# A softmax with relative position bias: chunks of three rows in eight buffers for chunks of four in six, and one store near the end issued later

## The chip, the cores and the metric

The kernel runs on one core of one Trainium2 chip. The metric is the device time of one execution in microseconds (us), lower is better. The core has five engines with instruction queues of their own; here VectorE (DVE in the profile) adds, inverts and scales, ScalarE (ACT) does the exponentials and issues the stores, SyncE (SP) issues the loads, GpSimd (POOL) makes two small index tables. Sixteen DMA engines carry out the transfers of both queues: loads on queue q1, stores on queue q10.

## The reference

```python
B, H, S = (2, 8, 2112); max_rel = 16
rel = clip(pos[:, None] - pos[None, :], -16, 16) + 16
logits = logits + rel_bias[:, rel][None]        # (2, 8, 2112, 2112) fp32
logits = logits - logits.max(axis=-1, keepdims=True)
exp = np.exp(logits)
out = exp / exp.sum(axis=-1, keepdims=True)
```

Each of the 2 x 8 x 2112 rows of 2112 numbers gets a bias that depends only on column minus row, clipped to 16 either way, and then a softmax over the row. 285.5 MB are read and as many written.

## The kernel before

**Tiling.** The rows are spread over 128 partitions: each of the 16 (batch, head) pairs has 8 partitions, and each partition has T = 264 rows that follow one another in memory. A chunk is R = 4 rows of every partition, one contiguous run of 4 x 8448 = 33,792 bytes in each. There are N = 66 chunks. BUFS = 6 buffers `L[u]` hold them; chunk n is in buffer n % 6, is changed in place and is stored from there. The bias comes from one strip `F` of 2375 numbers per partition, made once at the start: row after row reads it at an offset one smaller.

**What happens to a chunk.** SP issues the load (`load`, line 91), which counts up `loaded[u]` by 16 when it has landed. DVE waits for that (`vec`, line 126), adds the strip to rows 0 and 1 in one instruction and to rows 2 and 3 in a second (`add`, line 116; HALF = 2). After each, ACT does two exponentials whose sums go to `tot[u]` (`exps`, line 123). DVE waits for a pair's sums, takes the reciprocals (line 137) and scales the two rows (line 141), then the other pair. It counts up `scaled` once per chunk. ACT, which has gone on to `store` (line 95) after its fourth exponential, waits for `scaled` and issues the store, which counts up `stored[u]`. SP waits for `stored[u]` before it loads chunk n + 6 into the same buffer (`reload`, line 99). No row maximum is subtracted.

**What sets the order.** Every engine goes through the chunks in order, in a hardware loop of BUFS chunks per pass (`passes`, line 145) and the remainder unrolled. All waits are semaphores written out by hand: `take` (line 87) waits and subtracts. ACT's queue therefore reads: exponentials of n, wait for the scaling of n, store n, exponentials of n + 1. DVE's reads: wait for load n, both adds of n, wait for sums, first pair, wait for sums, second pair, wait for load n + 1.

**Start and end.** Chunk 0 is loaded in pieces (four quarters of row 0, then single rows; `FIRST`, line 66), so that the first bytes come early. The last buffer serves as scratch for making the strip, so its first load waits for `made`. The last chunk, 65, is loaded in two halves with a semaphore each (line 231), and DVE and ACT store it in two halves too; in `vec`, both adds of that chunk still come ahead of both scalings. SP ends by waiting for the last stores.

Of the kernel before, what the change touches and what calls it, by code (L numbers as in the profile page):

```python
# [14 lines left out]
def kernel(  # L15
# [18 lines left out]
    P = 128  # L34
    B, H, S, S2 = logits.shape
# [4 lines left out]
    T = S // Q  # L40
    assert Q * B * H == P and T * Q == S and T % W == 0
    M = T // W
    R = 4
    HALF = 2
    BUFS = 6
    N = T // R
    assert N * R == T
    FW = S + T - 1
    NB = (FW - 2 * MR) // W
    assert NB * W + 2 * MR == FW  # L50
    RS = R * S

    const = ctx.enter_context(tc.tile_pool(name="const", bufs=1))
    F = const.tile([P, FW], FP32, tag="F", name="F")
    rbP = const.tile([P, W], FP32, tag="rbP", name="rbP")
    L = [const.tile([P, RS], FP32, tag=f"L{u}", name=f"L{u}") for u in range(BUFS)]
    tot = [const.tile([P, R], FP32, tag=f"tot{u}", name=f"tot{u}") for u in range(BUFS)]


    qi, mm, qm, eq, lt, gt, rest = (  # L60
        L[BUFS - 1][:, NB * m : NB * (m + 1)] for m in range(7)
    )
# [3 lines left out]
    FIRST = [(S * m // 4, S * (m + 1) // 4) for m in range(4)]  # L66
    FIRST += [(S * m, S * (m + 1)) for m in range(1, R)]

    def rows(t, start, run=RS):
        return bass.AP(  # L70
            tensor=t.tensor, offset=t.offset + start * S, ap=[[T * S, P], [1, run]]
        )

    section = ctx.enter_context(tc.tile_critical(name="rows"))  # L74
    loaded = [nc.alloc_semaphore(f"loaded{u}") for u in range(BUFS)]
    stored = [nc.alloc_semaphore(f"stored{u}") for u in range(BUFS)]
    table = nc.alloc_semaphore("table")
    blocks_ready = nc.alloc_semaphore("blocks_ready")
    strip = nc.alloc_semaphore("strip")
    late = nc.alloc_semaphore("late")  # L80
# [6 lines left out]
    def take(eng, sem, v):  # L87
        eng.wait_ge(sem, v).then_inc(sem, -v)  # L88

    def load(eng, u, start):  # L90
        eng.dma_start(out=L[u][:], in_=rows(logits, start)).then_inc(loaded[u], 16)

    def store(eng, u, start, r0=0, r1=R):
        take(eng, scaled, 1)
        eng.dma_start(
            out=rows(out, start + r0, (r1 - r0) * S), in_=L[u][:, r0 * S : r1 * S]
        ).then_inc(stored[u], 16)

    def reload(eng, u, start):
        take(eng, stored[u], 16)  # L100
        load(eng, u, start)

    def add(eng, u, s0, start):
        x = L[u]
        x3 = bass.AP(
            tensor=x.tensor,
            offset=x.offset + (s0 + HALF - 1) * S,
            ap=[[list(x.ap[0])[0], P], [-S, HALF], [1, S]],
        )

        F3 = bass.AP(
            tensor=F.tensor,
            offset=(F.offset + T - HALF - s0) - start,
            ap=[[list(F.ap[0])[0], P], [1, HALF], [1, S]],
        )
        eng.tensor_tensor(out=x3, in0=x3, in1=F3, op=ALU.add).then_inc(added, 1)  # L116

    def exps(eng, u):
        for s0 in range(0, R, HALF):
            take(eng, added, 1)  # L120
            for i in range(s0, s0 + HALF):
                x = L[u][:, i * S : (i + 1) * S]
                e = eng.activation(out=x, in_=x, func=EXP, accum_out=tot[u][:, i : i + 1])  # L123
            e.then_inc(summed, 1)

    def vec(eng, u, start, halves=()):

        if not halves:
            take(eng, loaded[u], 16)
        for h, s0 in enumerate(range(0, R, HALF)):  # L130
            if halves:
                take(eng, halves[h], 16)
            add(eng, u, s0, start)
        for s0 in range(0, R, HALF):
            take(eng, summed, 1)
            t = tot[u][:, s0 : s0 + HALF]
            eng.reciprocal(out=t, in_=t).then_inc(inverted, 1)  # L137
            take(eng, inverted, 1)
            for i in range(s0, s0 + HALF):
                x = L[u][:, i * S : (i + 1) * S]  # L140
                e = eng.tensor_scalar_mul(out=x, in0=x, scalar1=tot[u][:, i : i + 1])  # L141
            if halves or s0 + HALF == R:
                e.then_inc(scaled, 1)

    def passes(eng, n0, n1, body):

        k = (n1 - n0) // BUFS * BUFS
        with eng.Fori(n0 * R, (n0 + k - BUFS) * R + 1, BUFS * R) as i:
            for u in range(BUFS):
                body((n0 + u) % BUFS, i + u * R)  # L150
        for n in range(n0 + k, n1):
            body(n % BUFS, n * R)
# [44 lines left out]
    def table_load(eng, bs):  # L197
        for b in bs:
            eng.dma_start(
                out=rbP[b * H * Q : (b + 1) * H * Q],  # L200
                in_=bass.AP(
                    tensor=rel_bias.tensor,
                    offset=rel_bias.offset,
                    ap=[[W, H], [0, Q], [1, W]],
                ),
            ).then_inc(table, 16)

    with nc.Block() as block:  # L208

        @block.sync  # L210
        def _(eng):


            for c0, c1 in FIRST:
                eng.dma_start(
                    out=L[0][:, c0:c1],
                    in_=bass.AP(
                        tensor=logits.tensor,
                        offset=logits.offset + c0,
                        ap=[[T * S, P], [1, c1 - c0]],  # L220
                    ),
                ).then_inc(loaded[0], 16)
            for u in range(1, BUFS):
                if u == BUFS - 1:
                    take(eng, made, 1)
                load(eng, u, u * R)
            passes(eng, BUFS, N - 1, lambda u, start: reload(eng, u, start))
            u = (N - 1) % BUFS
            take(eng, stored[u], 16)
            for s0, sem in ((0, loaded[u]), (HALF, late)):  # L230
                eng.dma_start(
                    out=L[u][:, s0 * S : (s0 + HALF) * S],
                    in_=rows(logits, (N - 1) * R + s0, HALF * S),
                ).then_inc(sem, 16)
            for n in range(N - BUFS, N - 1):
                take(eng, stored[n % BUFS], 16)
            take(eng, stored[u], 16 * R // HALF)

        @block.gpsimd
        def _(eng):  # L240
            eng.iota(qi, pattern=[[0, NB]], base=0, channel_multiplier=M).then_inc(  # L241
                blocks_ready, 1
            )
            eng.iota(mm, pattern=[[1, NB]], base=1 - M, channel_multiplier=0).then_inc(  # L244
                blocks_ready, 1
            )

        @block.scalar
        def _(eng):
            table_load(eng, range(B))  # L250

            def whole(u, start):
                exps(eng, u)
                store(eng, u, start)

            whole(0, 0)
            passes(eng, 1, N - 1, whole)
            u = (N - 1) % BUFS
            exps(eng, u)
            for s0 in range(0, R, HALF):  # L260
                store(eng, u, (N - 1) * R, s0, s0 + HALF)

        @block.vector
        def _(eng):
            strip_of(eng)
            eng.wait_ge(loaded[0], 16 * len(FIRST)).then_inc(loaded[0], 16 - 16 * len(FIRST))
            passes(eng, 0, N - 1, lambda u, start: vec(eng, u, start))
            u = (N - 1) % BUFS
            vec(eng, u, (N - 1) * R, halves=(loaded[u], late))


# [28 lines left out]
```

## Time and profile before

| | |
|---|---|
| Median of 6 runs | 1337.84 us |
| Lowest and highest | 1330.35 and 1351.61 us |
| Profiled execution, device time | 1355.03 us |
| Its span in the profile | 1353.3 us |
| DVE busy | 954.9 us, 539 instructions |
| ACT busy | 529.5 us, 529 instructions |
| Bytes moved | 571.00 MB, 422 GB/s over the span |
| ACT waiting for DVE ahead of exponentials | 788.4 us in 130 waits |
| DVE waiting ahead of adds | 262.5 us in 61 waits |

The times in the profile come from one execution. Its page gives busy time per engine, the span in 40 equal slices of 33.8 us (the busy share of an engine as a digit, and the GB/s that the DMA engines moved), the DMA queues with packets, megabytes and share of time, groups of equal instructions (line, engine, operation, output and input, count; busy us, mean ns of one; idle time just before them and who ended it), and the DMA issues (count, KB each, median us from issue to landing). A timeline lists instructions with start and duration. A table of stretches gives for each window its width, the busy time of DVE, ACT and POOL, the clock, the mean busy share of the 16 DMA engines and the GB/s. The trace behind it also holds a record of each DMA packet: queue, start, duration and bytes. A packet here is one partition's run of a chunk, or the 4-byte write that counts up a semaphore at the end of a transfer on each of the 16 DMA engines.

### The profile page before, as it was taken

Reading aid. Unit: us, or ns where it says so; the run is one execution under the profiler, and the core shown is the slowest. Engines: PE = TensorE matmul, PEld = TensorE weight load, DVE = VectorE, ACT = ScalarE, POOL = GpSimd, SP = SyncE. Lnnn points to the kernel's source line nnn. Section 1 sums busy time; section 2 is a strip of 40 time slices with the busy share of each in tenths; the row PEclk is TensorE's granted clock in tenths of the full one; section 3 lists DMA queues with packets and bytes.
Section 4 is the critical chain, followed back from the end, with each engine's and each line's share of the span. In section 5 each row is a group of like instructions: output and inputs, shape, how many; then the busy total and the mean of one; then the engine's idle time right before and its main releaser. Section 6 shows DMA issues by size and latency. Waiting matters only on the chain. (4 is left out here: it accounts for less than half of the span.)

```text
span 1353.3 us, 2505 instructions
## 1 busy us (share of the span) xinstructions
DVE 954.9 (71%) x539; ACT 529.5 (39%) x529; POOL 0.5 (0%) x6
## 2 busy tenths in 40 slices
DVE  6887766767767767667667767667667667667673
ACT  2444424424434334334334344244244344244242
POOL 0000000000000000000000000000000000000000
DMA  9999999999999999999999999999999999999975
GB/s 387 428 432 433 432 432 433 430 432 432 429 427 433 428 430 432 427 430 428 430 428 430 430 433 431 431 432 431 434 433 432 434 435 431 427 431 432 428 328 238
DMA packets 20307, 571.00 MB, mean 422 GB/s; under 512 B 2384, under 2 KB 2384, under 8 KB 2896
## 3 DMA queue, kind: packets, MB, share of 16 engines
q1 hardware_dynamic: 10512, 285.48, 49.6%
q10 hardware_dynamic: 9792, 285.50, 48.9%
q14 instruction: 3, 0.02, 0.0%
HBM read 285.49 MB, written 285.47 MB: 422 GB/s over the span
## 5 line engine op out<-in xcount | busy, mean ns | idle before, releaser
L123 ACT ACTIVATE L<-L 128x2112 f32<-128x2112 f32 x264 | 516.0, 1955 | 788.4 <-ACTq L88 788.4
L116 DVE TENSOR_TENSOR L<-L,F 128x4224 f32<-128x4224 f32 x132 | 595.8, 4555 | 262.5 <-DVEq L88 262.5
L141 DVE TENSOR_SCALAR L<-L,tot 128x2112 f32<-128x2112 f32 x264 | 336.4, 1316 | 20.0 <-DVEq L88 3.0
L137 DVE RECIPROCAL tot<-tot 128x2 f32<-128x2 f32 x132 | 21.3, 162 | 99.1 <-DVEq L88 99.1
L123 ACT ACTIVATION_READ_ACCUMULATOR L<-L 128x1 f32 x264 | 49.2, 186 | 0.0
L123 ACT ACT_TABLE_LOAD x1 | 1.3, 1283 | 21.6 <-ACTq L88 21.6
L193 DVE TENSOR_TENSOR F<-L,rbP 128x2343 f32<-128x2343 f32 x1 | 2.6, 2601 | 0.1
L194 DVE TENSOR_TENSOR F<-F,L 128x2343 f32<-128x2343 f32 x1 | 2.6, 2600 | 0.1
L185 DVE TENSOR_SCALAR L<-L,rbP 128x71 f32<-128x71 f32 x1 | 0.3, 259 | 3.1 <-DVEq L88 3.1
L180 DVE TENSOR_SCALAR L<-L 128x71 int32<-128x71 int32 x1 | 0.2, 199 | 1.5 <-DVEq L88 1.5
L183 DVE TENSOR_SCALAR L<-L 128x71 f32<-128x71 f32 x3 | 0.6, 198 | 0.5 <-DVEq L88 0.2
L188 DVE SCALAR_TENSOR_TENSOR L<-L,rbP 128x71 f32<-128x71 f32 x1 | 0.3, 294 | 0.2 <-DVEq L88 0.2
L181 DVE TENSOR_TENSOR L<-L 128x71 f32<-128x71 int32 x1 | 0.2, 234 | 0.1
L186 DVE COPY F<-rbP 128x16 f32<-128x16 f32 x1 | 0.2, 175 | 0.1
L192 DVE COPY F<-rbP 128x16 f32<-128x16 f32 x1 | 0.2, 176 | 0.1
L244 POOL IOTA L<- 128x71 int32 x1 | 0.2, 189 | 0.0
L241 POOL IOTA L<- 128x71 int32 x1 | 0.2, 188 | 0.6 <-SPq L74 0.6
L284 POOL MEMSET const-bfloat16-1.0<- 128x1 bf16 x1 | 0.1, 102 | 0.0
L284 POOL MEMSET const-uint8-127<- 128x1 uint8 x1 | 0.1, 102 | 0.0
L284 POOL MEMSET const-float32-0.0<- 128x1 f32 x1 | 0.1, 99 | 0.2 <-issue 0.2
L284 POOL MEMSET const-float32-1.0<- 128x1 f32 x1 | 0.1, 99 | 0.0
## 6 DMA issues: line engine op xcount, KB each, us to landing
out_dram<-L ACTq DMA_DIRECT2D x65, 4224.0 KB, 47.1
L<-in_logits_dram SPq DMA_DIRECT2D x64, 4224.0 KB, 58.4
L<-in_logits_dram SPq DMA_DIRECT2D x2, 2112.0 KB, 60.5
out_dram<-L ACTq DMA_DIRECT2D x2, 2112.0 KB, 9.0
L<-in_logits_dram SPq DMA_DIRECT2D x3, 1056.0 KB, 10.0
L<-in_logits_dram SPq DMA_DIRECT2D x4, 264.0 KB, 3.4
rbP<-in_rel_bias_dram ACTq DMA_DIRECT2D x2, 8.2 KB
```

The costliest lines, as they stand in the source:

```text
L116: eng.tensor_tensor(out=x3, in0=x3, in1=F3, op=ALU.add).then_inc(added, 1)
L123: e = eng.activation(out=x, in_=x, func=EXP, accum_out=tot[u][:, i : i + 1])
L137: eng.reciprocal(out=t, in_=t).then_inc(inverted, 1)
L141: e = eng.tensor_scalar_mul(out=x, in0=x, scalar1=tot[u][:, i : i + 1])
L180: step(eng.tensor_single_scalar(out=qi, in_=qi, scalar=M * Q - 1, op=ALU.bitwise_and))
L181: step(eng.tensor_tensor(out=qm, in0=qi, in1=mm, op=ALU.subtract))
L183: step(eng.tensor_scalar(out=m, in0=qm, scalar1=0.0, scalar2=None, op0=op))
L185: step(eng.tensor_scalar(out=rest, in0=lt, scalar1=low, scalar2=None, op0=ALU.mult))
L188: eng.scalar_tensor_tensor(out=rest, in0=gt, scalar=high, in1=rest, op0=ALU.mult, op1=ALU.add)
L193: step(eng.tensor_tensor(out=blocks, in0=wide(eq), in1=rev, op=ALU.mult))
L194: step(eng.tensor_tensor(out=blocks, in0=blocks, in1=wide(rest), op=ALU.add))
L284: nc = _bacc.Bacc("TRN2", target_bir_lowering=False, num_devices=1)
```

## The change

Chunks have three rows in place of four, so there are 88 of them, in eight buffers in place of six. The two halves of a chunk become `PARTS`: rows 0 and 1, and row 2 alone. Adds, exponentials, reciprocals and scalings follow these parts, and so do the two loads and two stores of the last chunk.

At the end ACT's order is written out. Up to chunk 84 it is as before. The store of chunk 85 (the last but two) isn't issued after its own exponentials: it is handed to `exps` of chunk 86 as `first` and issued there after the wait for chunk 86's first add and ahead of its first exponential. Then follow the store of 86, the exponentials of 87 and its two stores.

```diff
-    R = 4
-    HALF = 2
-    BUFS = 6
+    R = 3
+    PARTS = [(0, 2), (2, R)]
+    BUFS = 8
...
-    def exps(eng, u):
-        for s0 in range(0, R, HALF):
+    def exps(eng, u, first=None):
+        for r0, r1 in PARTS:
             take(eng, added, 1)
-            for i in range(s0, s0 + HALF):
+            if first and r0 == 0:
+                first()
+            for i in range(r0, r1):
...
-        for h, s0 in enumerate(range(0, R, HALF)):
-            if halves:
-                take(eng, halves[h], 16)
-            add(eng, u, s0, start)
-        for s0 in range(0, R, HALF):
+        for m, (r0, r1) in enumerate(PARTS):
+            if parts:
+                take(eng, parts[m], 16)
+            add(eng, u, r0, r1, start)
+        for r0, r1 in PARTS:
             take(eng, summed, 1)
-            t = tot[u][:, s0 : s0 + HALF]
+            t = tot[u][:, r0:r1]
...
-            for s0, sem in ((0, loaded[u]), (HALF, late)):
+            for (r0, r1), sem in zip(PARTS, (loaded[u], late)):
...
-            passes(eng, 1, N - 1, whole)
-            u = (N - 1) % BUFS
+            passes(eng, 1, N - 3, whole)
+
+            u = (N - 3) % BUFS
             exps(eng, u)
-            for s0 in range(0, R, HALF):
-                store(eng, u, (N - 1) * R, s0, s0 + HALF)
+            exps(eng, (N - 2) % BUFS, lambda: store(eng, u, (N - 3) * R))
+            store(eng, (N - 2) % BUFS, (N - 2) * R)
+            exps(eng, (N - 1) % BUFS)
+            for r0, r1 in PARTS:
+                store(eng, (N - 1) % BUFS, (N - 1) * R, r0, r1)
```

More of the change, by code (lines that the diff above doesn't have):

```diff
@@ L101, in reload, with add @@
         load(eng, u, start)
-    def add(eng, u, s0, start):
+    def add(eng, u, r0, r1, start):
         x = L[u]
@@ L106, in add @@
             tensor=x.tensor,
-            offset=x.offset + (s0 + HALF - 1) * S,
-            ap=[[list(x.ap[0])[0], P], [-S, HALF], [1, S]],
+            offset=x.offset + (r1 - 1) * S,
+            ap=[[list(x.ap[0])[0], P], [-S, r1 - r0], [1, S]],
         )
@@ L112, in add @@
             tensor=F.tensor,
-            offset=(F.offset + T - HALF - s0) - start,
-            ap=[[list(F.ap[0])[0], P], [1, HALF], [1, S]],
+            offset=(F.offset + T - r1) - start,
+            ap=[[list(F.ap[0])[0], P], [1, r1 - r0], [1, S]],
         )
         eng.tensor_tensor(out=x3, in0=x3, in1=F3, op=ALU.add).then_inc(added, 1)
-    def exps(eng, u):
-        for s0 in range(0, R, HALF):
+    def exps(eng, u, first=None):
+        for r0, r1 in PARTS:
             take(eng, added, 1)
-            for i in range(s0, s0 + HALF):
+            if first and r0 == 0:
+                first()
+            for i in range(r0, r1):
                 x = L[u][:, i * S : (i + 1) * S]
@@ L124, in exps, with vec @@
             e.then_inc(summed, 1)
-    def vec(eng, u, start, halves=()):
-        if not halves:
+    def vec(eng, u, start, parts=()):
+        if not parts:
             take(eng, loaded[u], 16)
-        for h, s0 in enumerate(range(0, R, HALF)):
-            if halves:
-                take(eng, halves[h], 16)
-            add(eng, u, s0, start)
-        for s0 in range(0, R, HALF):
+        for m, (r0, r1) in enumerate(PARTS):
[3 more added lines that the diff above has]
+        for r0, r1 in PARTS:
             take(eng, summed, 1)
-            t = tot[u][:, s0 : s0 + HALF]
+            t = tot[u][:, r0:r1]
             eng.reciprocal(out=t, in_=t).then_inc(inverted, 1)
             take(eng, inverted, 1)
-            for i in range(s0, s0 + HALF):
+            for i in range(r0, r1):
                 x = L[u][:, i * S : (i + 1) * S]
                 e = eng.tensor_scalar_mul(out=x, in0=x, scalar1=tot[u][:, i : i + 1])
-            if halves or s0 + HALF == R:
+            if parts or r1 == R:
                 e.then_inc(scaled, 1)
@@ L229, in _ @@
             take(eng, stored[u], 16)
-            for s0, sem in ((0, loaded[u]), (HALF, late)):
+            for (r0, r1), sem in zip(PARTS, (loaded[u], late)):
                 eng.dma_start(
-                    out=L[u][:, s0 * S : (s0 + HALF) * S],
-                    in_=rows(logits, (N - 1) * R + s0, HALF * S),
+                    out=L[u][:, r0 * S : r1 * S],
+                    in_=rows(logits, (N - 1) * R + r0, (r1 - r0) * S),
                 ).then_inc(sem, 16)
@@ L236, in _ @@
                 take(eng, stored[n % BUFS], 16)
-            take(eng, stored[u], 16 * R // HALF)
+            take(eng, stored[u], 16 * len(PARTS))
         @block.gpsimd
@@ L268, in _ @@
             u = (N - 1) % BUFS
-            vec(eng, u, (N - 1) * R, halves=(loaded[u], late))
+            vec(eng, u, (N - 1) * R, parts=(loaded[u], late))
 _INS = ['logits', 'rel_bias']
```

## The prediction

> **What bounds the kernel now.** I read the page's busy shares first, then its 40 slices, its queues and issue groups, then stretches of the end, and the timeline at both ends.
>
> ```profile
> DVE 954.9 (71%) x539; ACT 529.5 (39%) x529; POOL 0.5 (0%) x6
> DMA  9999999999999999999999999999999999999975
> GB/s 387 428 432 433 432 432 433 430 432 432 429 427 433 428 430 432 427 430 428 430 428 430 430 433 431 431 432 431 434 433 432 434 435 431 427 431 432 428 328 238
> q1 hardware_dynamic: 10512, 285.48, 49.6%
> q10 hardware_dynamic: 9792, 285.50, 48.9%
> out_dram<-L ACTq DMA_DIRECT2D x65, 4224.0 KB, 47.1
> L<-in_logits_dram SPq DMA_DIRECT2D x64, 4224.0 KB, 58.4
> ```
>
> No engine is full, but the transfers are: 36 slices lie between 427 and 435 GB/s. Loads (q1) and stores (q10) move 571 MB. Loads take 58.4 us from issue to landing and stores 47.1, though one chunk each way passes in 20.4 us (load 6 is issued at 58.6 us, load 65 at 1262.5: 1203.9/59), so 5.2 chunks of transfers are always outstanding. The chain of waits stops after 2.6 us and says nothing.
>
> The two weak slices look like loss: (432-328)/432 and (432-238)/432 of 33.8 us are 8.1 + 15.2 = 23 us. Stretches of the end (width; DVE, ACT, POOL busy; clock; DMA share; GB/s) show whose loss it is:
>
> ```profile
> 1297.00:1317.00 20.00, 14.42 (x9) 8.01 (x8) 0.00 (x0) 1.00 0.66 279
> 1317.00:1325.00 8.00, 4.41 (x1) 3.47 (x3) 0.00 (x0) 1.00 0.95 410
> 1325.00:1331.00 6.00, 0.23 (x1) 0.53 (x2) 0.00 (x0) 1.00 0.50 214
> 1331.00:1335.00 4.00, 4.00 (x1) 0.00 (x0) 0.00 (x0) 1.00 0.06 25
> 1335.00:1338.00 3.00, 2.85 (x4) 2.55 (x3) 0.00 (x0) 1.00 0.08 34
> ```
>
> A share of 0.06 is one DMA engine of 16. In the packet records that engine finishes load 64 at 1300.3 us and the two halves of load 65 at 1315.3 and 1330.3; another is through with them at 1297.6. From 1299 on the late one has no gap: it has eight packets of store 64 left at 1331.6, which last to 1341.5, when store 65's first half (issued 1338.21) is waiting; that takes it to 1346.5, the second half (issued 1342.56) to 1351.5. **The bound is one late DMA engine, busy to the end; the 23 us belong to the other fifteen**, which cannot take over its partitions.
>
> Its own work: a 33,792 B packet takes 1251 ns and the next starts 4 ns before its end, 1247 ns; 16,896 B take 625, 8448 B 315, 2112 B 82 ns in the same way. Per engine: 1032 x 1.247 + 32 x 0.625 + 24 x 0.315 + 32 x 0.082 + 140 completion writes x 0.006 = 1318 us. The first packet starts at 2.0 us, the span ends 1.8 us after the last, 1.7 us lie around the span: **1323.5 us with no packet late**. The profiled execution took 1355.0 (span 1353.3), so its late engine lost 31 us to slow packets, spread over the run (20.4 us per chunk against 16 x 1.247 = 19.95). The median, 1337.84, is 17 below the profiled execution: about 14 us lost.
>
> **The Trainium skill.** "DMA: Bandwidth & Descriptors", section "Where 436 GB/s comes from", puts the ports' ceiling at 435 GB/s; the slices agree (427 to 435). Its section "Queues, rings and completion order" says that each DMA engine takes its queues in turn, packet by packet; the records alternate so wherever both have work. Its section "Latency and other measured facts" says that two engines are usually slower, and suspects GpSimd-issued DMAs; here one is late although none is issued by GpSimd. "VectorE: DVE Perf Modes", section on the TRN2 errata, prices an fp32 tensor_tensor at (N+151)/0.96 ns: 4557 for N = 4224, where the row below has 4555.
>
> **The change part by part.**
>
> *Bytes and packets.* Bytes are the same. A 25,344 B packet lies on the line through the sizes above: 1247 - (1247-315)/3 = 936 ns. Per engine then 1384 x 0.936 (86 loads, 87 stores, 8 packets each) + 16 x 0.625 + 32 x 0.315 + 32 x 0.082 + 183 x 0.006 = 1319 to 1320: **+1 to +2 us**, on the path. Bounds: nothing, if the line is flat, and +7 if slow packets come per packet and not per byte (a third more of some 14 us is +5, added to the +2).
>
> *Compute per chunk.* It must stay below the DMA period, about 0.75 x 20.4 = 15.3 us (14.98 with no packet late).
>
> ```profile
> L123 ACT ACTIVATE L<-L 128x2112 f32<-128x2112 f32 x264 | 516.0, 1955 | 788.4 <-ACTq L88 788.4
> L116 DVE TENSOR_TENSOR L<-L,F 128x4224 f32<-128x4224 f32 x132 | 595.8, 4555 | 262.5 <-DVEq L88 262.5
> L141 DVE TENSOR_SCALAR L<-L,tot 128x2112 f32<-128x2112 f32 x264 | 336.4, 1316 | 20.0 <-DVEq L88 3.0
> L137 DVE RECIPROCAL tot<-tot 128x2 f32<-128x2 f32 x132 | 21.3, 162 | 99.1 <-DVEq L88 99.1
> 50.03 9.02 DVE L116 TENSOR_TENSOR L<-L,F 128x4224 f32<-128x4224 f32 x2
> 66.11 9.02 DVE L116 TENSOR_TENSOR L<-L,F 128x4224 f32<-128x4224 f32 x2
> ```
>
> The last two lines, where DVE never waits for data, give 16.08 us per chunk of four, against 20.4: 4.3 spare. For three rows: two-row add 4.55, hand-over 0.13, two exponentials to 8.7, hand-over 0.14, reciprocal and its wait 0.31, two scalings to 11.6; the one-row add (2357 ns by the formula) fits under the exponentials; the third exponential ends at 10.8, under the scalings; reciprocal and one scaling to **13.2**. Spare: 1.8 to 2.1 us. DVE's sum goes from 955 to 88 x (4.555 + 2.357 + 3 x 1.316 + 2 x 0.162) = 984 us. Cost nothing: covered by the transfers. With the cover gone it would be the rival below.
>
> *Eight buffers of three.* The same 24 rows. In-flight time is 8 x 15.3 - 13.5 = 109 us, before 6 x 20.4 - 16.4 = 106. It splits otherwise. Chunk 0 is in about 2.5 us sooner (14.4) and its store goes out near 28.5 instead of 33.9, so fewer loads have landed by then; when store 0 lands (about 48), 4.2 of 8 loads are in, and the next load waits for 3.8 + 1 chunks: near 70 us for loads, 39 for stores (58 and 47 before). Both queues stay filled; cost nothing. DMA issues (0.35 us each on ACT, 88 in place of 66) lie in ACT's idle time. In the first stretch six small loads go out instead of seven: nothing, the engines are busy behind them.
>
> *The held store.* Chunks 85 to 87 end the run. Store 85's wait for the scaling and its one DMA issue move on ACT behind the wait for chunk 86's first add. Take load 86's landing as 0. Chunk 85's scaling ends near -1.9; the store now goes out at 4.9, **7 us later**. Queued behind it on ACT are the exponentials of 86 (+0.35 us, in DVE's spare time), and nobody waits for stored[5] but SP's last waits, since the last load needs store 79. On its own queue it overtakes nothing, and q1 is not touched. A gap opens only if the late engine runs out of stores before 4.9. Store 84 went out at -17.3 and would land at +21.7, so about 10 packets are left at 0; the two-row load takes 8 of them past by 12.5 us (936 + 625 ns a pair) and they last to about 15. Then 85 and 86 (out at 13.7) are there. The last load is in at 22.5, with 10 store packets left, to 31.9; the two-row part's store is out at 29.2, the last at 30.8. **No gap before, none after: gain 0.** Bounds: -3 us if in the shown runs the margin of 3.3 us with which store 65's first half came in time (1338.2 against 1341.5) is missing, +5 if the store queue is empty at 0, when the store is held.
>
> Sum: +1.5 + 0 + 0 + 0. Against the profiled execution 1355.0 + 1.5; carried to the median, **1339 us**.
>
> **Rivals.**
>
> 1. *The ending is repaired.* If in the shown runs, unlike the profiled one, all sixteen engines stand still together for part of the 23 us, letting loads go first and a shorter last part fill it. For it: the two weak slices. Against it: the late engine has no gap, and the fastest run shown, 1330.35, is only 7 us above the 1323.5. The most it can reach is 1323.5 + 1.5 = 1325 with no late packet at all; likely 1331.
>
> 2. *Compute becomes the bound (slower).* Place: DVE's chunk of 13.2 us. If the two hand-overs per chunk, now with one row behind the second, don't overlap as I laid them, the third exponential, its hand-over, reciprocal and scaling come after the rest: 13.2 + 2.1 = 15.3, and with each 0.5 us more, 88 x 0.5 = 44 us. It decides from 15.0 us per chunk on: at 15.3, 88 x 15.3 plus a head of 14 and a tail of 15 give 1375. Against it: the 16.08 us period shows every hand-over at 0.1 to 0.15 us.
>
> 3. *Late packets come per packet.* Then the 14 us become 19 in the median: 1344; for over 1% slower they would have to double.
>
> **How the numbers follow.** A measurement of this kernel can tell about 1% from no change (the six runs span 1330.35 to 1351.61). Forecast 0.68 (1332 to 1348, the scatter of the late engine's loss); ending repaired 0.12 (1331); per-packet loss 0.14 (1344, up to 1354); compute bound 0.06 (1375). Faster by over 1% means below 1324.5, under the floor of 1325 unless the kernel before is measured higher than here: 0.05. Slower by over 1% is above 1351: the compute case and about half of the per-packet case with its scatter, 0.12. Within 1%: 0.83. The range 1329 to 1352 leaves out the compute case and the outer scatter.
>
> **What will show it.** Right: slices still at 427 to 435 GB/s, about a third more packets, loads near 70 us and stores near 39 to landing, DVE still waiting at its first add each chunk, a chunk period near 13.2 us where it doesn't wait, and at the end a stretch with a DMA share near 0.06 while the late engine is never without work. Wrong: DVE's wait at the first add gone (rival 2); a share near 1.0 to within 10 us of the end and a lower time (rival 1); more slow packets on the late engine (rival 3).

## The result and the profile after

The changed kernel takes 1333.21 us in the median of 34 runs (1332.0 to 1334.68). Against the kernel before, run beside it, the ratio is 0.9992, with a 95% interval of 0.9979 to 1.0006: no change that can be told. The ratio leaves out executions over 1.5% above the fastest of their kernel, and the profiled execution of before, 1355.03 us, is one of these. Over all 71 executions of before in these runs the median is 1342.84, as they scatter from 1329.2 to 1366.76; those of the changed kernel lie within 2.7 us. The profiled execution of the changed kernel took 1332.41 us, its span is 1330.6.

From the page of the changed kernel, in the order of the lines shown of before (busy shares; 40 slices of 33.3 us; the two queues; issues with us to landing):

```profile
DVE 968.1 (73%) x627; ACT 524.8 (39%) x529; POOL 0.5 (0%) x6
DMA  9999999999999999999999999999999999999998
GB/s 381 431 433 432 433 432 434 431 433 433 433 433 432 434 432 434 432 434 432 433 433 433 432 434 430 435 430 435 430 434 431 434 430 434 431 434 431 433 432 348
q1 hardware_dynamic: 13536, 285.48, 50.0%
q10 hardware_dynamic: 12960, 285.50, 49.8%
out_dram<-L ACTq DMA_DIRECT2D x87, 3168.0 KB, 43.1
L<-in_logits_dram SPq DMA_DIRECT2D x86, 3168.0 KB, 62.7
```

The plateau is where it was, 430 to 435 GB/s, with nearly a third more packets. DVE and ACT are about as idle as before. What differs is the end. Stretches of it in the changed kernel (width; DVE, ACT, POOL busy; clock; DMA share; GB/s):

```profile
1295.00:1300.00 5.00, 4.85 (x5) 0.56 (x2) 0.00 (x0) 1.00 1.00 427
1305.00:1310.00 5.00, 2.75 (x3) 2.17 (x3) 0.00 (x0) 1.00 1.01 433
1310.00:1315.00 5.00, 3.63 (x4) 1.64 (x2) 0.00 (x0) 1.00 1.01 436
1315.00:1320.00 5.00, 0.00 (x0) 0.00 (x0) 0.00 (x0) 1.00 0.98 419
1320.00:1325.00 5.00, 0.00 (x0) 0.00 (x0) 0.00 (x0) 1.00 0.81 345
1325.00:1330.60 5.60, 0.00 (x0) 0.00 (x0) 0.00 (x0) 1.00 0.05 23
```

All sixteen DMA engines work until about 1320 us. The stretch in which one engine works alone, some 7 us before (1331 to 1338), is missing. The packet records show a difference that goes with it. I call a packet late if it takes over 4% longer than the usual (median) time of its size; packets under 8 KB are left out. The excess is the time that all these packets, late or not, took over their usual times, summed over the sixteen engines. In the profile of before 614 of 17,408 packets are late and the excess is 149 us; in the profile of the changed kernel 31 of 22,912 are late, with 13 us. The two executions are not alike, though: that of before lay 26 us above its kernel's lowest time. An execution of four rows at 1333.78 us (hold_r4 below) has 218 late packets and an excess of 33 us. A 25,344-byte packet takes 940 ns, and on the average of 11,008 loads 940.5.

DVE's rows after, from the page (idle time and its cause last), and its first unhindered chunks on the timeline:

```profile
L116 DVE TENSOR_TENSOR L<-L,F 128x4224 f32<-128x4224 f32 (+1 forms) x176 | 600.8, 3455 | 134.9 <-DVEq L88 134.9
L139 DVE RECIPROCAL tot<-tot 128x2 f32<-128x2 f32 (+1 forms) x176 | 28.3, 161 | 175.5 <-DVEq L88 175.5
42.93 6.82 DVE L116 TENSOR_TENSOR L<-L,F 128x4224 f32<-128x4224 f32 x2
56.07 4.55 DVE L116 TENSOR_TENSOR L<-L,F 128x4224 f32<-128x4224 f32 x1
```

A chunk is 13.14 us here (42.93 to 56.07). DVE's wait ahead of the adds has shrunk from 262.5 to 134.9 us, which is from 4.0 to 1.5 us per chunk, and the spare time with it; it is not gone.

### The profile page after: what moved, and what is told of

Read it like the earlier page. It is cut to its first block, busy times and chain, and to the rows that moved or that the text cites. A ratio compares the mean times of both kernels' runs of the same rounds, so it can differ in the third digit from the quotient of the medians.

```text
span 1330.6 us, 3010 instructions
## 1 busy us (share of the span) xinstructions
DVE 968.1 (73%) x627; ACT 524.8 (39%) x529; POOL 0.5 (0%) x6
## 5 line engine op out<-in xcount | busy, mean ns | idle before, releaser
L116 DVE TENSOR_TENSOR L<-L,F 128x4224 f32<-128x4224 f32 (+1 forms) x176 | 600.8, 3455 | 134.9 <-DVEq L88 134.9
L143 DVE TENSOR_SCALAR L<-L,tot 128x2112 f32<-128x2112 f32 x264 | 340.4, 1318 | 28.2 <-DVEq L88 6.7
L139 DVE RECIPROCAL tot<-tot 128x2 f32<-128x2 f32 (+1 forms) x176 | 28.3, 161 | 175.5 <-DVEq L88 175.5
## 6 DMA issues: line engine op xcount, KB each, us to landing
out_dram<-L ACTq DMA_DIRECT2D x87, 3168.0 KB, 43.1
L<-in_logits_dram SPq DMA_DIRECT2D x86, 3168.0 KB, 62.7
```

## The experiments

Theory: the sixteen DMA engines bound the kernel, each with its own share of packets; the shape of the chunks and the held store matter only through the cost per packet and through gaps in which both queues are empty. Rivals: the held store gives something and the smaller chunks take it; compute takes over with smaller chunks; late packets, of which the profile of before had so many, come per packet. All runs are in the table, with the ratio to the kernel before run beside them. The last two columns come from one profiled execution each.

| Run | rows x buffers | median us (lowest to highest) | ratio, 95% interval | late packets, excess us | late from 100 to 1250 us |
|---|---|---|---|---|---|
| changed kernel again | 3 x 8 | 1333.22 (1331.94 to 1334.49) | 0.9962 [0.9939, 0.9985] | 86, 28 | 1 |
| no_hold | 3 x 8 | 1333.14 (1331.22 to 1334.06) | 0.9959 [0.9934, 0.9983] | 61, 23 | 1 |
| hold_long | 3 x 8 | 1337.26 (1335.85 to 1338.68) | 0.9997 [0.9966, 1.0029] | 92, 30 | 1 |
| hold_r4 | 4 x 6 | 1343.06 (1330.09 to 1362.94) | 0.9997 [0.9959, 1.0034] | 218, 33 | 110 |
| r6_b4 | 6 x 4 | 1338.77 (1335.59 to 1341.9) | 1.0017 [0.9992, 1.0042] | 244, 111 | 36 |
| r2_b12 | 2 x 12 | 1338.24 (1337.64 to 1339.49) | 1.0008 [0.9986, 1.003] | 105, 24 | 2 |
| r3_b6 | 3 x 6 | 1332.99 (1331.26 to 1335.03) | 0.9959 [0.9936, 0.9982] | 93, 29 | 0 |
| r4_split | 4 x 6 | 1370.88 (1367.56 to 1371.36) | 1.0242 [1.019, 1.0294] | 1454, 486 | 1241 |
| r4_split_both | 4 x 6 | 1337.3 (1335.68 to 1338.52) | 0.9994 [0.9969, 1.0019] | 81, 19 | 1 |
| r4_b4 | 4 x 4 | 1333.55 (1331.49 to 1341.19) | 0.9962 [0.9937, 0.9987] | 216, 48 | 121 |
| r3_rows_first | 3 x 8 | 1332.26 (1330.87 to 1334.74) | 0.9943 [0.9918, 0.9969] | 104, 30 | 1 |
| r2_pair | 2 x 12 | 1558.12 (one run) | none taken | 5119, 1613 | 4093 |

In the last column before has 478 and the changed kernel 1. The medians are over all executions of a run. The changed kernel stands at 0.9992 and, once more, at 0.9962 of the kernel before, so such a difference between two ratios comes from the scatter of before and says nothing of a change. The first four rows of the table were measured on one chip, the next four on a second, the last four on a third. The kernel before ran on all three and scatters there by 40, 36 and 39 us, while the medians of three rows agree within 1 us, so medians can be compared across them to about that.

**The two parts of the change, apart.** The changed kernel once more:

> The changed kernel once more, beside the other three. Theory (transfers bound it, per-packet cost alone moves it): 1332 to 1335 us, 1 to 3 us above the lowest times of the kernel before. Rival (three rows cost more, the held store gives it back): the same here; the next two runs tell them apart.

The median is as expected. The lowest time is 3.5 us above the lowest of before in these runs (1331.94 against 1328.4), a little more than the 1 to 3 us expected.

Three rows without the held store:

```diff
-            passes(eng, 1, N - 3, whole)
-            u = (N - 3) % BUFS
-            exps(eng, u)
-            exps(eng, (N - 2) % BUFS, lambda: store(eng, u, (N - 3) * R))
-            store(eng, (N - 2) % BUFS, (N - 2) * R)
+            passes(eng, 1, N - 1, whole)
             exps(eng, (N - 1) % BUFS)
```

> Three rows in eight buffers, every store in its old place. Theory: within 1 us of the changed kernel (1332 to 1335 us), since the DMA engines have store packets left whenever the store is held. Rival (the held store gives something back): 3 to 8 us above the changed kernel. Store of chunk 85 issued about 6 us earlier than in the changed kernel, after chunk 85's last scaling.

Four rows with the held store:

```diff
-    R = 3
-    PARTS = [(0, 2), (2, R)]
-    BUFS = 8
+    R = 4
+    PARTS = [(0, 2), (2, 4)]
+    BUFS = 6
```

> Four rows in six buffers, with only the store of the last chunk but two held back. Theory: same as the kernel before within 1 us, and 1 to 2 us below the changed kernel at the lowest times. Rival (the held store gives something): 3 to 8 us below the kernel before.

With and without it three rows take 1333.22 and 1333.14 us; with it four rows stand at 0.9997 of four rows without. On three rows the held store moves nothing. On four rows no effect can be told either, but the interval leaves room for 0.4%, some 5 us, and the 3 to 8 us of the rival aren't wholly excluded there. That the store is held at all is seen on the timelines, first of the changed kernel and then of the kernel without the hold (start, duration, instruction):

```profile
1281.37 1.32 DVE L143 TENSOR_SCALAR L<-L,tot 128x2112 f32<-128x2112 f32 x1
1284.48 6.83 DVE L116 TENSOR_TENSOR L<-L,F 128x4224 f32<-128x4224 f32 x2 [1.79 <-DVEq L88]
1289.22 0.34 ACTq L95 DMA_DIRECT2D out_dram<-L  x1
1289.61 1.96 ACT L125 ACTIVATE L<-L 128x2112 f32<-128x2112 f32 x1 [9.53 <-ACTq L88]
```

```profile
1283.10 1.32 DVE L143 TENSOR_SCALAR L<-L,tot 128x2112 f32<-128x2112 f32 x1
1284.53 0.34 ACTq L95 DMA_DIRECT2D out_dram<-L  x1
1286.21 6.83 DVE L116 TENSOR_TENSOR L<-L,F 128x4224 f32<-128x4224 f32 x2 [1.78 <-DVEq L88]
```

In the first the store goes out 6.5 us after the scaling's end (1282.69), in the second 0.1. Meanwhile the DMA share of the changed kernel stays at 1.00:

```profile
1282.00:1290.00 8.00, 6.21 (x3) 0.39 (x1) 0.00 (x0) 1.00 1.00 431
```

The end of hold_r4 shows what the prediction had ruled out, a gap before the last stores, in an execution that took 1333.78 us:

```profile
1297.00:1317.00 20.00, 10.06 (x5) 6.80 (x7) 0.00 (x0) 1.00 0.77 332
1317.00:1325.00 8.00, 2.71 (x3) 1.20 (x2) 0.00 (x0) 1.00 0.96 408
```

In the first stretch 0.23 x 20 = 4.6 us are lost on the average of the engines: the last two rows are added from 1309.52 to 1314.08 us, and the first store after that goes out at 1316.96. The changed kernel and no_hold have no such gap. The hold is not what closes it, since hold_r4 has the hold and no_hold has none. Whether the last part of one row does is not shown: r4_split_both, below, has a last part of two rows, smaller packets, and no gap either. Over the last 40 us of transfers the engines are idle for 7.0 us on the average in hold_r4 and for 4.0 in the changed kernel. By that, closing the gap is worth some 3 us, an estimate. The lowest times don't show it: hold_r4's is 1330.09 us, the changed kernel's 1331.94.

**When holding costs.** The stores of 85 and 86 both after the last exponentials:

```diff
-            u = (N - 3) % BUFS
-            exps(eng, u)
-            exps(eng, (N - 2) % BUFS, lambda: store(eng, u, (N - 3) * R))
-            store(eng, (N - 2) % BUFS, (N - 2) * R)
-            exps(eng, (N - 1) % BUFS)
+            for n in range(N - 3, N):
+                exps(eng, n % BUFS)
+            for n in range(N - 3, N - 1):
+                store(eng, n % BUFS, n * R)
```

> As the changed kernel, but the stores of chunks 85 and 86 both held back until all exponentials of chunk 87 are done. Theory (holding costs exactly the time in which both transfer queues are empty): store 84 and the last loads are through near 1298 to 1300 us, the exponentials end near 1308, so the DMA engines stand still for 6 to 10 us and the run takes 1339 to 1343 us. Rival (it does good that the last loads go alone): below 1333 us.

It costs 4.0 us, and 1337.26 us is below the 1339 to 1343 expected. The stretches of that run:

```profile
1295.00:1300.00 5.00, 4.85 (x5) 1.11 (x2) 0.00 (x0) 1.00 1.02 436
1300.00:1305.00 5.00, 3.18 (x1) 1.70 (x1) 0.00 (x0) 1.00 0.42 176
1305.00:1310.00 5.00, 4.04 (x4) 4.02 (x5) 0.00 (x0) 1.00 0.19 81
1310.00:1315.00 5.00, 2.33 (x3) 0.34 (x2) 0.00 (x0) 1.00 1.01 431
```

Here the engines stand still for 0.58 x 5 + 0.81 x 5 = 7 us on the average, where I expected it. The time grew by less than that. After the gap the engines end closer together: from 1310 us on they are idle for 2.5 us on the average here (shares 1.01, 1.07, 0.89 and, from 1325 to 1334.5, 0.75), in the changed kernel for 6.3. So more than half of the 7 us is won back at the end, and a mean over the engines overstates what the last one loses.

**Larger and smaller chunks.** As hold_r4, with `R = 6`, parts `[(0, 3), (3, 6)]`, `BUFS = 4`:

> Six rows in four buffers, parts of three rows, the last store but two held as in the changed kernel. Theory: per-packet cost falls by under 1 us, but the last part now has three rows: add 6.8, exponentials 6.1, scalings 4.3 us after its landing, while only about 4 us of store packets are left, so a gap of 5 to 8 us opens: lowest times 1334 to 1339 us. Rival (larger chunks are simply cheaper): below 1330 us.

The lowest time, 1335.59 us, is in the range expected; the median is 5.6 us above that of three rows. Its stretches show a gap at the end that the hold did not open, as the held store goes out at 1268.59 us:

```profile
1300.00:1310.00 10.00, 0.62 (x1) 0.00 (x0) 0.00 (x0) 1.00 1.00 433
1310.00:1315.00 5.00, 5.00 (x1) 0.00 (x0) 0.00 (x0) 1.00 0.26 112
1315.00:1320.00 5.00, 4.85 (x5) 3.75 (x3) 0.00 (x0) 1.00 0.00 0
1320.00:1325.00 5.00, 2.65 (x4) 2.20 (x4) 0.00 (x0) 1.00 0.92 390
```

From about 1311 to 1320 us the engines have almost nothing: the last part, three rows, is added from 1309.38 to 1316.14, and the part ahead of it is scaled only after that. As almost no store is left to cover it, 0.74 x 5 + 5 = 8.7 us are lost. That is more than the 5 to 8 us expected, since I had left about 4 us of stores where almost none were. The gap is not all that sets this run apart: of its excess of 111 us, 85 fall ahead of 100 us, where a slice falls to 389 GB/s, so its time doesn't measure the gap alone.

With `R = 2`, parts `[(0, 1), (1, 2)]`, `BUFS = 12`:

> Two rows in twelve buffers, parts of one row. Theory: packets of 16,896 bytes cost +3 to +4 us against the kernel before, DVE needs about 8.4 us per chunk of 10.0, so still hidden: 1333 to 1337 us. Rival (compute takes over as chunks shrink): above 1345 us, and DVE no longer waits for loads.

1338.24 us, 5 above three rows and 1 us more than the top of what I expected; where that last us goes was not traced. Compute doesn't take over: DVE still waits 179.9 us ahead of its adds. With the same two rows as one part, `PARTS = [(0, 2)]`, it does:

> Two rows in twelve buffers as one part, so that nothing runs beside the exponentials of a chunk on DVE: 4.55 + 0.13 + 4.0 + 0.14 + 0.31 + 2.5 = 11.6 us per chunk against 10.0 us of transfers. Theory (compute takes over above the transfers' period): 132 x 11.6 + a head of 14 and a tail of 10 us, 1545 to 1565 us, DVE never waiting for loads after the start. Rival (the exponentials overlap the next chunk): below 1400 us.

DVE's timeline in the middle of that run:

```profile
711.89 4.55 DVE L116 TENSOR_TENSOR L<-L,F 128x4224 f32<-128x4224 f32 x1
720.71 0.17 DVE L139 RECIPROCAL tot<-tot 128x2 f32<-128x2 f32 x1 [4.27 <-DVEq L88]
721.02 2.55 DVE L143 TENSOR_SCALAR L<-L,tot 128x2112 f32<-128x2112 f32 x2
723.49 4.55 DVE L116 TENSOR_TENSOR L<-L,F 128x4224 f32<-128x4224 f32 x1
```

723.49 - 711.89 = 11.60 us, against 10 us of transfers; the wait of 4.27 us for the exponentials has nothing beside it. 1558 us lies within the 1545 to 1565 expected. So compute, the prediction's second rival, does take over once a chunk's compute is longer than its transfers; with three rows it is shorter.

**Fewer buffers.** The changed kernel with `BUFS = 6`:

> Three rows in six buffers, 18 rows in place of 24. Theory: transfers outstanding fall from 107 to about 77 us in sum, still some five chunks, both queues stay filled: same as the changed kernel within 1 us, 1332 to 1335. Rival (the eight buffers carry the result): slower by over 1%, DMA share below 0.98 in the middle of the run.

1332.99 us: the same, with 18 rows in place of 24. Loads there take 37.4 us to landing and stores 38.8, and the plateau stays at 429 to 436 GB/s.

**Where the late packets come from.** The kernel before, its loads halved:

```diff
-        eng.dma_start(out=L[u][:], in_=rows(logits, start)).then_inc(loaded[u], 16)
+        for r in range(0, R, HALF):
+            eng.dma_start(
+                out=L[u][:, r * S : (r + HALF) * S], in_=rows(logits, start + r, HALF * S)
+            ).then_inc(loaded[u], 16)
...
-            take(eng, loaded[u], 16)
+            take(eng, loaded[u], 16 * R // HALF)
...
```

> The kernel before, its 4-row loads issued as two loads of two rows each (packets of 16,896 bytes in place of 33,792), stores as they were. Theory: 512 packets of 1.247 us per engine become 1024 of 0.625, +1.5 us, so the lowest times near 1331 to 1332 us. If the late engine of the profile of before comes with large load packets, its late packets go and the times lie close together; if lateness comes per packet (rival 3 of the prediction), there is more of it.

A clear miss: 1370.88 us, a ratio of 1.0242 with an interval of 1.019 to 1.0294, the slowest of all but r2_pair. From its page:

```profile
L<-in_logits_dram SPq DMA_DIRECT2D x130, 2112.0 KB, 77.1
out_dram<-L ACTq DMA_DIRECT2D x65, 4224.0 KB, 19.9
```

In the packet records the two queues take turns by packet where both have work, so loads with half the packet get half the bytes of a turn. The stores then run out first: with the records put together into engines by their starts and ends, as well as these tell, 8128 loads between 100 and 1250 us are followed by another load and 6317 by a store, against 2604 and 12,056 when both queues have equal packets (the next run). The wait has moved into the loads (77.1 us; stores 19.9, one chunk's passage). And late packets are many, 1454, on both queues: a 16,896-byte load takes 650 ns on the average, where it takes 630 in r2_b12. So small load packets alone are no cure. Stores halved in the same way as well, so that all packets have 16,896 bytes and the chunks still four rows (the loads as above; the waits for `stored` count both transfers):

```diff
-        eng.dma_start(
-            out=rows(out, start + r0, (r1 - r0) * S), in_=L[u][:, r0 * S : r1 * S]
-        ).then_inc(stored[u], 16)
+        for r in range(r0, r1, HALF):
+            eng.dma_start(
+                out=rows(out, start + r, HALF * S), in_=L[u][:, r * S : (r + HALF) * S]
+            ).then_inc(stored[u], 16)
```

> Four rows in six buffers as before, but loads and stores both issued as two transfers of two rows, so that all packets have 16,896 bytes, as in the kernel of two rows in twelve buffers. Theory A (late packets come from unlike packets, 16.9 KB against 33.8 KB, or from large ones): as two rows in twelve buffers, 1335 to 1340 us, and about 6 us of late time over all engines. Theory B (they come with chunks of four rows, whatever the packets): late time of 50 us and more over all engines, and times that differ by over 10 us.

This is theory A: 81 late packets, one of them between 100 and 1250 us, and 1337.3 us, about as two rows in twelve buffers. The excess, 19 us, is above the 6 expected; 14 of it fall ahead of 100 us. So it is not the four rows of a chunk but how they are transferred. Packets and transfers were halved together (a transfer has 128 packets in every run), so which of the two counts is not told apart. The amount outstanding, with `BUFS = 4` in the kernel before and nothing else:

> The kernel before with four buffers in place of six, nothing else. Transfers outstanding fall from 106 to about 4 x 20.2 - 16.4 = 64 us. Theory (transfers bound it while both queues stay filled): the lowest times as before, 1329 to 1332 us. If the late packets come with the amount outstanding, they go and the times lie close together; if with the four rows, they stay.

In between: 216 late packets, 48 us, times 9.7 us apart, lowest 1331.49. Less outstanding did not remove the late packets. But the times of the kernel before beside it lie 39 us apart (1328.92 to 1367.88), and the median, 1333.55, is about that of the changed kernel, so the scatter hangs on the amount outstanding too.

In the profiles of the kernels that transfers bound, then, those whose packets all have 25,344 bytes or fewer have at most 105 late ones, and at most 2 between 100 and 1250 us. Those with packets of 33,792 bytes or more on some queue have at least 216, and 36 to 1241 in that stretch. Size alone doesn't make a packet late: r2_pair, with none above 16,896 bytes, has 5119, nearly all after 200 us, where compute holds its transfers back to some 370 GB/s. And the excess of hold_r4, 33 us, is hardly above the 30 of hold_long, most of which falls ahead of 100 us. What in the chip makes a packet late is open; it was not tried further.

**The start.** Chunk 0 in whole rows:

```diff
-    FIRST = [(S * m // 4, S * (m + 1) // 4) for m in range(4)]
-    FIRST += [(S * m, S * (m + 1)) for m in range(1, R)]
+    FIRST = [(S * m, S * (m + 1)) for m in range(R)]
```

> The changed kernel with chunk 0 loaded in three whole rows, without the quarters of row 0. Theory: the first packets (2112 bytes, 102 to 121 ns on the average in the profiles where 86 is the usual time) cost about 1 us: 1331.5 to 1334 us, within what can be told. Rival (the start holds the 7 us that the run lies above its packets' sum): below 1330 us.

1332.26 us, in the range expected and the lowest median of all, 1 us below the changed kernel's 1333.22. The two were measured on different chips, so that 1 us is not shown to come from the start.

## Why the prediction was right, point by point

**The verdict** (within 1%, 1339 us, range 1329 to 1352) held: 1333.21 us and a ratio of 0.9992. That the number came within 6 us is partly luck, since two terms were off in opposite ways (the last two points).

**The signs.** The plateau, the number of packets, DVE's wait at the first add and the chunk period came as forecast. (The slices of before at 427 to 435 GB/s are 37, not 36.) The stretch with a share near 0.06 at the end did not come: the share stays near 1.0 until 1320 us, some 10 us from the end, and the time is lower, which the prediction had named as the sign of rival 1.

**What bounds it.** Shown: the DMA engines. Buffers (r3_b6) and the order of stores (no_hold) could be changed without moving the time, and DVE's spare time could shrink to 1.5 us per chunk; a gap in the queues (hold_long) moved it, and so did the packets (r4_split against r4_split_both).

**Compute per chunk.** 13.2 us predicted, 13.14 measured. The one-row add, 2357 ns by the formula, took 2352 on the average. DVE's sum, 984 predicted, is 968: I added instructions at full length, where neighbours overlap: two adds take 6.83 us and not 6.91, two scalings 2.55 and not 2.64, and the next add starts 0.09 us before the last scaling ends. Over 88 chunks that is some 23 us less; the strip's 7 us, which I had left out, come on top.

**Time in flight.** Near 70 us for loads and 39 for stores predicted, 62.7 and 43.1 measured. Their sum, 109 predicted, is 106. The split was mis-sized, without effect.

**The held store.** 7 us later predicted, 6.5 measured; gain 0 for three rows: shown by no_hold. "No gap before" was true of the profiled execution, where the late engine has none, but not of the execution of hold_r4, which loses 4.6 us in one.

**Rival 1**, a repaired ending, fell as far as the held store goes, but not altogether: its sign came, and the gap of four rows is closed with three. Some 3 us, the estimate above, is as much as the prediction's bound of -3 us. No run here tests a shorter last part alone. **Rival 2**, compute, needs a chunk above its transfers, as r2_pair has; three rows don't. **Rival 3**, late packets per packet, is contradicted: nearly a third more packets than in hold_r4, and between 100 and 1250 us 1 late against 110.

**The term that was mis-sized** is the last step, "carried to the median, 1339". I took the late engine's loss, some 14 us in the median, over unchanged, with a bound on one side only, that it might grow; that it might go stood under rival 1 alone, at 1325 to 1331 us. The step's own rule, lateness per byte or per packet, was wrong for these kernels. With packets of 25,344 bytes the loss is nearly gone: the excess per engine is 13/16 = 0.8 us in the mean, up to 30/16 = 1.9 in the other three-row runs. Nor were the 14 us late packets alone: hold_r4's execution of 1333.78 us lies 10 us above the 1323.5, but its late packets explain 33/16 = 2.1 us in the mean and its gap 4.6. That the bound was one late engine was true of the profiled execution of before; it is not true of the changed kernel.

**The sum without lateness** was too low in turn: 1323.5 + 1.5 = 1325 against the 1332.4 of the profiled execution. Of these 7 us about 2 are lost at the start: by 15 us the changed kernel has moved 4 x 142 + 6 x 325 + 5 x 448 GB/s x us, worth 11.0 us at 433 GB/s, so 4.0 are gone where I counted 2.0. The end loses about 4.5: from 1320 on the shares 0.81 and 0.05 leave 0.95 + 5.3 us, of which I had counted 1.8, because the engines end up to 5 us apart. Late packets, 0.8 us, make up the rest. So a lateness some 13 us too large and a start and end some 6.5 us too small went into the same 1339: that they partly cancel is luck. The lowest times of four rows (1329.2) and of three (1332.0) differ by 2.8 us, where +1 to +2 was predicted for the packets.

## What to carry to other kernels

Where transfers bound a kernel, look at the DMA share in short stretches of the end before you believe that a weak last slice can be filled: 0.06 of sixteen engines is one engine at work. Look at more than one execution, too: that of before ended with one late engine, that of hold_r4 with a gap for most of them. In these runs a store could be held, or two buffers dropped, without cost as long as the queues kept packets; the price began when the last part's compute was longer than the stores still left. And a loss that one profiled execution shows need not belong to the work: ask which property of the transfers it hangs on before you carry it over to a kernel that changes just that.

## What the runs showed of the hardware

- Where transfers bound the kernel, late packets went with large packets. Loads of 33,792 bytes averaged 1266 ns in the profile of before (1355.03 us), with a usual time of 1251 and a longest of 2605, and 1251.5 in that of hold_r4 (1333.78 us); loads of 25,344 bytes averaged 940.5 with a usual time of 940. From 100 to 1250 us there were 478, 110 and 1 late packets in these three.
- Small packets can be late too: 5119 of r2_pair's, where compute held the transfers back, none above 16,896 bytes.
- Packets of unlike size on the two queues made the longest time of the kernels that transfers bound: 16,896-byte loads beside 33,792-byte stores took 1370.88 us, the same bytes with 16,896 on both 1337.3.
- The cost per packet is small: 2112 bytes take 86 ns, 8448 take 319, 16,896 take 629, 25,344 take 940, 33,792 take 1251. All lie near 8 ns and 27.2 bytes per ns, and the next packet starts some 3 to 4 ns before the end.
